# The unit of the attention scores moves into the split of queries and keys; tables are used as loaded

## The chip, the cores and the metric

The kernel runs on one core of one Trainium2 chip. A core has five engines that each follow their own list of instructions in order: TensorE (PE in the profile, with its weight loads as PEld), VectorE (DVE), ScalarE (ACT), GpSimd (POOL) and SyncE (SP), which here issues nearly all DMAs. The metric is device time of one execution in microseconds, the median of the timed runs; lower is better.

## The reference

Two inputs, a prompt of 512 rows and a sample of 1024 rows of width 1024, pass through the same encoder layer. What matters here is its attention part, 8 heads of width 64:

```python
h = rmsnorm(x, n_pre)
aq, ak, av, gq, gk, gv, gr, glr = jnp.split(h @ w_in, IN_OFFSETS, axis=-1)
o_attn = dilated_attention(heads(aq), heads(ak), heads(av))   # three (window, dilation) pairs
#   s = q . k / 8 - slope[h] * |distance|;  softmax of each branch, branches merged by their denominators
o_gla = gla_mixer(gq, gk, gv, gr, glr, ...)                   # gated linear attention beside it
x = x + rmsnorm(concat(o_attn, o_gla) @ w_out, n_post)
# then: h = rmsnorm(x); gelu(depthwise conv(h @ w_up[a])) * (h @ w_up[g]) @ w_down; rmsnorm; residual add
```

The three branches share keys. The kernel computes one softmax over all keys with a table per head that holds slope times distance, less the logarithm of the number of branches that see the key, and 1e30 where none does. Keys that lie outside the sequence, which the reference counts with score zero, enter as one more column, from the table `miss`.

## The kernel before

**Numbers.** A float32 product is made of three products of halves: an operand x becomes hi = fp16(x * f) and lo = fp16(x * f - hi), with a factor f, and `mm3` (lines 343 to 345) adds hi*hi, hi*lo and lo*hi in one PSUM bank. The factors of the weights are powers of two that are measured on the chip: a `Group` of four weight units gets the sum of its squares (`measure`, one ScalarE pass over each unit at line 245), then `finish` makes the factor `scale` with a small TensorE product (line 252), a VectorE sum (253), and GpSimd and VectorE operations on one column. `undo` is what turns a product back into plain numbers; call it u. Queries and keys left the projection as product times the constant `-PART` or `PART` (2 to the -15), so that their product was a score in the unit u * u / PART**2 / 8 of its head pair. The tables of distances and `miss` were divided by that unit on GpSimd, once per head (lines 553 and 556), and the exponential took the unit as its scale, and `top`, the row's extreme times the unit (line 211), as its bias.

**Stages.** The prompt is projected first (`main1`: 12 column blocks in feature-major form, then 6 in token-major form), while the samples' rows are normed beside it. Then the samples are projected (`main2`) while the prompt's attention and linear attention run beside it (`mixers(0, ...)`); then the output projection and the gated MLP of the prompt, with the samples' `mixers(1, ...)` beside the MLP; then the samples' output projection and MLP, which fill the last third of the time. `_weave` sets how many steps of the side work go between the steps of the main work.

**Order.** The program is written as if in one stream, and a scheduler then places each engine's instructions, so that the order on an engine is that of the built program and not of the source. DMAs go out on SP's queue in its order.

**Weights.** `_Weights` takes the weights in units of [128, 512] elements; two units make a load of 512 KB (line 92) into one of six buffers. Before unit i is used, its hi (line 111, ScalarE) and lo (line 120, VectorE) have been made, and the units ahead of it loaded and measured. `ahead(0)`, called with the first row tile, loaded 10 units in five DMAs and measured 8 of them. The first blocks are `inproj_lead`: two blocks by two half-widths, 96 products of 128x256.

**The first rows.** `norm_T` loads a tile of 128 rows, sums its squares (line 368), norms it (398), transposes it on TensorE (405) and splits it into hi and lo, `c` (348 and 353). After the last load come the small tables in SP's order: `gg` (line 1154, a row of 64 numbers spread over 128 partitions and 8 heads), `cf`, which VectorE casts to `cm` (1159), `ph_sb` (the table `miss`), the masks (one of them cast at 1167) and `cvt`.

**Attention.** `attention` handles its heads in a pipeline of steps: `scores` (two matmuls per piece, 583 and 584), one step later `reduce` (VectorE, 597: adds the table to the scores in PSUM, writes `t` and keeps the row's minimum `m`), then `expo` (ScalarE, 610), `part_hi` (reciprocal 618, GpSimd `rs` 619, ScalarE `p` 622), `part_lo` (VectorE, 629), `turn` (a DMA that transposes, 638), `pv` (665) and `out` (674 to 680). `load(h)` brings a head's table (549), queries (559) and keys (561), `load_v` its values; there are two sets of buffers, and head h + 2 is loaded once the scores of head h are reduced. The prompt has 4 row tiles per head and two `t` buffers, the samples 8 and three.

Of the kernel before, what the change touches and what calls it, by code (L numbers as in the profile page):

```python
# [69 lines left out]
class _Weights:  # L70
# [78 lines left out]

    def next(self):  # L150
        i = self.i
        self.flush(i)
        self._finish()
        self._upto("hi", self._hi, i + self.HI)
        self._upto("lo", self._lo, i + self.LO)
        self.ahead(i + 1)
        self.i += 1
        return self.parts.pop(i)
# [3 lines left out]
def encoder(ctx, tc, xp, xs, n_pre, w_in, wg, g_gla, w_out, n_post, n_ffn_pre, w_up, conv, w_down,  # L162
# [65 lines left out]
    class Group:  # L228
# [4 lines left out]
        def __init__(self, nm, n, rows, *more, scores=False):  # L233
# [3 lines left out]
            self.scores = const.tile([128, 3], F32, name=f"scores_{nm}") if scores else None  # L237
# [12 lines left out]
        def finish(self):  # L250
# [10 lines left out]
            if self.scores is not None:  # L261
                c = [self.scores[:, i:i + 1] for i in range(3)]
                times(c[0], u, u)
                times(c[0], c[0], PART ** -2 / 8.0)
                times(c[1], c[0], -1.0)
                nc.vector.reciprocal(out=c[2], in_=c[0])
# [19 lines left out]
    G_FM = [Group(f"fm{i}", 4, r_pre, scores=i < 4) for i in range(6)]  # L286
# [137 lines left out]
    def store_fm(c, i, ps):  # L424
        seq, o0 = where(c)
        m = FM_ORDER[i]
        if m < 8:
            t = tmp.tile([128, 2, CH], FP16, name="stq", tag="two")
            split_psum(ps, t[:, 0], t[:, 1], -PART if m < 4 else PART)
# [105 lines left out]
    def attention(seq):  # L535
# [5 lines left out]
        nbuf = 2  # L541
        with ExitStack() as es:
# [4 lines left out]
            def load(h):  # L547
# [4 lines left out]
                unit = G_FM[h // 2].scores[:, 2:3]  # L552
                nc.gpsimd.tensor_scalar(out=bias, in0=bias, scalar1=unit, scalar2=3e38, op0=ALU.mult, op1=ALU.min)
                miss = hp.tile([128, nkt], F32, name="miss", tag="miss")
                m0 = seq * 32 + h * nkt
                nc.gpsimd.tensor_scalar(out=miss, in0=ph_sb[:, m0:m0 + nkt], scalar1=unit, scalar2=3e38,
                                        op0=ALU.mult, op1=ALU.min)
# [5 lines left out]
                heads[h] = (bias, qs, kk, miss)  # L563
# [15 lines left out]
            def scores(h, qt, k0, k1, last):  # L579
                _, qs, kk, _ = heads[h]  # L580
# [6 lines left out]
            def reduce(h, qt, k0, k1, last):  # L587
                bias, miss = heads[h][0], heads[h][3][:, qt:qt + 1]
# [15 lines left out]
            def expo(h, qt):  # L604
# [3 lines left out]
                s = G_FM[h // 2].scores  # L608
                top = times(up.tile([128, 1], F32, name="top", tag="top", bufs=4), m, s[:, 0:1])
                nc.scalar.activation(out=t[:, kf:], in_=t[:, kf:], func=ACTF.Exp, scale=s[:, 1:2], bias=top,  # L610
                                     accum_out=den)
# [530 lines left out]
    with ExitStack() as es:  # L1142
# [5 lines left out]
        def first():  # L1148
            g_pre.append(gain_row(stage, n_pre, "g0"))
            r_pre.set(g_pre[0])  # L1150
            W.ahead(0)
# [171 lines left out]
```

## Time and profile before

| | us |
|---|---|
| timed runs, median of 3 | 2120.15 (2115.74 to 2127.61) |
| profiled execution | 2108.8 |
| its span, first to last instruction | 2107.0 |
| TensorE busy in it | 1904.1 |
| VectorE, ScalarE, GpSimd busy | 1202.9, 975.8, 373.4 |

The mean granted clock of TensorE over the span was 0.964. The profiled execution was faster than each of the timed ones, so a sum made against its span says by how much the time moves; where the median then lies is read with the 11.35 us between the two in mind. In rows in order of time the first number is the start in us, the second the length of the row's instructions, and what stands in brackets is the idle time of the engine before it and what ended it. In rows of groups, the numbers behind the bar are busy us and mean ns of one, and behind the second bar the idle time before them. Rows by stretch give for each engine the busy us and, in parentheses, the number of instructions.

### The profile page before, as it was taken

Reading aid. Unit: us, or ns where it says so; the run is one execution under the profiler, and the core shown is the slowest. Engines: PE = TensorE matmul, PEld = TensorE weight load, DVE = VectorE, ACT = ScalarE, POOL = GpSimd, SP = SyncE. Lnnn points to the kernel's source line nnn. Section 1 sums busy time; section 2 is a strip of 40 time slices with the busy share of each in tenths; the row PEclk is TensorE's granted clock in tenths of the full one; section 3 lists DMA queues with packets and bytes.
Section 4 is the critical chain, followed back from the end, with each engine's and each line's share of the span. In section 5 each row is a group of like instructions: output and inputs, shape, how many; then the busy total and the mean of one; then the engine's idle time right before and its main releaser. Section 6 shows DMA issues by size and latency. Waiting matters only on the chain. (4 is left out here: it accounts for less than half of the span.)

```text
span 2107.0 us, 31702 instructions
## 1 busy us (share of the span) xinstructions
PE 1904.1 (90%) x11912; PEld 1184.5 (56%) x11912; DVE 1202.9 (57%) x2367; ACT 975.8 (46%) x1858; POOL 373.4 (18%) x657
## 2 busy tenths in 40 slices
PE   3999779999978886799899989989999999999996
PEld 2586334787853443454555557844655656464655
DVE  4554753432448786796756654675254554545456
ACT  5674554322447785686635433553422232314233
POOL 3212540000154443531011111210000000000002
PEclk9999789999999998899999999999999999999998
DMA  6666785335558999985424447641111211111132
GB/s 194 190 181 149 177 177 157 106 102 187 194 151 157 181 174 167 182 175 145 136 86 133 124 162 262 234 162 55 46 46 50 61 40 50 51 55 46 61 125 85
DMA packets 389615, 274.75 MB, mean 130 GB/s; under 512 B 173875, under 2 KB 342067, under 8 KB 389461
## 3 DMA queue, kind: packets, MB, share of 16 engines
q1 hardware_dynamic: 389460, 272.72, 48.1%
q8 instruction: 94, 1.54, 0.3%
q14 instruction: 61, 0.49, 0.1%
HBM read 191.83 MB, written 47.28 MB: 113 GB/s over the span
## 5 line engine op out<-in xcount | busy, mean ns | idle before, releaser
L343 PE MATMUL bank<-c,w_hi 128*128 128x512 f16 (+1 forms) x816 | 313.2, 384 | 16.8 <-ACT w_hi L111 9.4
L345 PE MATMUL bank<-c,w_lo 128*128 128x512 f16 (+1 forms) x816 | 312.0, 383 | 10.3 <-DVE w_lo L120 10.3
L344 PE MATMUL bank<-c,w_hi 128*128 128x512 f16 (+1 forms) x816 | 313.0, 384 | 0.0
L345 PEld LDWEIGHTS <-w_lo 128*128 128x128 f16 x1360 | 135.6, 100 | 175.0 <-DVE w_lo L120 14.5
L343 PEld LDWEIGHTS <-w_hi 128*128 128x128 f16 x1360 | 136.6, 100 | 170.0 <-issue 14.5
L344 PEld LDWEIGHTS <-w_hi 128*128 128x128 f16 x1360 | 135.7, 100 | 162.9 <-issue 19.3
L111 ACT ACTIVATE w_hi<-w_raw,up_up 128x512 f16<-128x512 f32 x176 | 125.6, 720 | 217.0 <-PE bank L344 108.9
L344 PE MATMUL bank<-w_lo,f 128*128 128x512 f32 x528 | 212.9, 403 | 9.5 <-DVE w_lo L118 9.2
L343 PE MATMUL bank<-w_hi,f 128*128 128x512 f32 x528 | 212.2, 409 | 3.1 <-DVE ya L1076 1.7
L345 PE MATMUL bank<-w_hi,f 128*128 128x512 f32 x528 | 211.3, 400 | 0.0
L111 ACT ACTIVATE w_hi<-w_raw 128x512 fp32r<-128x512 f32 x144 | 90.2, 630 | 243.6 <-PE bank L345 190.9
L120 DVE SCALAR_TENSOR_TENSOR w_lo<-w_raw,up_up,w_hi 128x512 f16<-128x512 f32 x176 | 134.6, 767 | 110.5 <-PE bank L345 54.0
L118 DVE TENSOR_TENSOR w_lo<-w_raw,w_hi 128x512 fp32r<-128x512 f32 x144 | 98.5, 688 | 117.2 <-PE bank L344 82.9
L972 POOL TENSOR_TENSOR small<-small 128x1 f32<-128x1 f32 x24 | 8.6, 357 | 812.2 <-ACT junk L368 812.2
L1042 DVE SCALAR_TENSOR_TENSOR ya<-bank,cvt,ya 128x511 f32<-128x511 f32 x176 | 107.9, 614 | 72.8 <-ACT ya L1044 66.6
L1112 DVE TENSOR_TENSOR y<-bank,y 128x512 f32<-128x512 f32 x144 | 96.5, 687 | 87.8 <-PE bank L345 87.6
L345 PE MATMUL bank<-d,w_lo 128*128 128x512 f16 x352 | 133.4, 379 | 1.5 <-DVE w_lo L120 1.5
L343 PE MATMUL bank<-d,w_hi 128*128 128x512 f16 x352 | 133.5, 379 | 0.1
L344 PE MATMUL bank<-d,w_hi 128*128 128x512 f16 x352 | 133.4, 379 | 0.0
L245 ACT ACTIVATE w_junk<-w_raw 128x512 bf16<-128x512 f32 (+1 forms) x136 | 85.3, 627 | 87.3 <-DMA w_raw<-in_w_up_dram 45.7
L344 PEld LDWEIGHTS bank<-w_lo,f 128*128 128x128 f32 x528 | 100.8, 191 | 34.8 <-DVE w_lo L118 13.6
L629 DVE SCALAR_TENSOR_TENSOR p<-t,rs,p 128x512 f16<-128x512 f32 (+2 forms) x96 | 91.2, 955 | 45.1 <-ACT p L622 44.5
(196 smaller groups left out, 3910.5 us busy)
## 6 DMA issues: line engine op xcount, KB each, us to landing
w_raw<-in_w_up_dram SPq DMA_DIRECT2D x88, 512.0 KB, 4.5
w_raw<-in_w_in_dram SPq DMA_DIRECT2D x44, 512.0 KB, 4.4
w_raw<-in_w_down_dram SPq DMA_DIRECT2D x36, 512.0 KB, 3.6
mix<-mx SPq DMA_DIRECT2D x24, 512.0 KB, 10.5
xin<-in_x_sample_dram SPq DMA_DIRECT2D x16, 512.0 KB, 5.1
w_raw<-in_w_out_dram SPq DMA_DIRECT2D x32, 256.0 KB, 6.2
xin<-x SPq DMA_DIRECT2D x16, 512.0 KB, 4.7
bias<-in_nbias_dram SPq DMA_DIRECT2D x8, 832.0 KB, 7.4
```

The costliest lines, as they stand in the source:

```text
L111: self.nc.scalar.activation(out=self.hi[i], in_=raw, func=ACTF.Copy, scale=1.0 if group is None else group.scale)
L118: self.nc.vector.tensor_tensor(out=lo, in0=raw, in1=hi.bitcast(F32), op=ALU.subtract)
L120: self.nc.vector.scalar_tensor_tensor(out=lo, in0=raw, scalar=group.scale, in1=hi, op0=ALU.mult, op1=ALU.subtract)
L245: nc.scalar.activation(out=junk[:, :raw.shape[1]], in_=raw, func=ACTF.Square, accum_out=self.sums[:, self.at:self.at + 1])
L343: nc.tensor.matmul(out, ah, bh, start=start, stop=False)
L344: nc.tensor.matmul(out, ah, bl, start=False, stop=False)
L345: nc.tensor.matmul(out, al, bh, start=False, stop=stop)
L629: nc.vector.scalar_tensor_tensor(out=p[:, n:2 * n], in0=t[:, kf:T], scalar=rs, in1=p[:, 0:n], op0=ALU.mult, op1=ALU.subtract)
L972: nc.gpsimd.tensor_tensor(out=r, in0=self.ss[0], in1=self.ss[1], op=ALU.add)
L1042: nc.vector.scalar_tensor_tensor(out=out, in0=src, scalar=cw[:, j:j + 1], in1=out, op0=ALU.mult, op1=ALU.add)
L1112: nc.vector.tensor_tensor(out=y[t][:, cols], in0=ps[t], in1=y[t][:, cols], op=ALU.add)
```

## The change

Queries and keys now leave the projection with factors of their own head pair in place of the constant: keys with k = min(u, PART), queries with q = -max(u / PART, 1) * u / 8, whose product is -u * u / 8, so that a score comes out in plain numbers (with its sign turned, as before). The tables of distances and `miss` are then used as they are loaded, the exponential has the scale -1.0 and the minimum `m` itself as bias, and the unit, the scaled `miss` tiles and `top` are gone. In the prompt's attention (one chunk) a head's buffers are three in place of two. At the start, `start` loads and measures the four units of the first group only, and makes its factor, with the first row tile; what `ahead(0)` did before is done when the first unit is asked for.

```diff
+    def start(self):
+        n = self.units[0][5].n
+        self._upto("load", self._load, n - 1)
+        self._upto("measure", self._measure, n - 1)
+        self._finish()
+
     def next(self):
         i = self.i
         self.flush(i)
         self._finish()
+        if i == 0:
+            self.ahead(0)
         self._upto("hi", self._hi, i + self.HI)
...
-            self.scores = const.tile([128, 3], F32, name=f"scores_{nm}") if scores else None
+            self.heads = const.tile([128, 2], F32, name=f"heads_{nm}") if heads else None
...
-            if self.scores is not None:
-                c = [self.scores[:, i:i + 1] for i in range(3)]
-                times(c[0], u, u)
-                times(c[0], c[0], PART ** -2 / 8.0)
-                times(c[1], c[0], -1.0)
-                nc.vector.reciprocal(out=c[2], in_=c[0])
+            if self.heads is not None:
+                k, q = (self.heads[:, i:i + 1] for i in range(2))
+                nc.gpsimd.tensor_scalar(out=k, in0=u, scalar1=PART, scalar2=None, op0=ALU.min)
+                nc.gpsimd.tensor_scalar(out=q, in0=u, scalar1=1.0 / PART, scalar2=1.0, op0=ALU.mult, op1=ALU.max)
+                nc.gpsimd.tensor_scalar(out=q, in0=q, scalar1=u, scalar2=-0.125, op0=ALU.mult, op1=ALU.mult)
...
-            split_psum(ps, t[:, 0], t[:, 1], -PART if m < 4 else PART)
+            f = G_FM[i // 2].heads
+            split_psum(ps, t[:, 0], t[:, 1], f[:, 1:2] if m < 4 else f[:, 0:1])
...
-        nbuf = 2
+        nbuf = 3 if nh == 1 else 2
...
                 kk = hp.tile([128, 2, T], FP16, name="kk", tag="kk")
-                unit = G_FM[h // 2].scores[:, 2:3]
-                nc.gpsimd.tensor_scalar(out=bias, in0=bias, scalar1=unit, scalar2=3e38, op0=ALU.mult, op1=ALU.min)
-                miss = hp.tile([128, nkt], F32, name="miss", tag="miss")
-                m0 = seq * 32 + h * nkt
-                nc.gpsimd.tensor_scalar(out=miss, in0=ph_sb[:, m0:m0 + nkt], scalar1=unit, scalar2=3e38,
-                                        op0=ALU.mult, op1=ALU.min)
...
-                bias, miss = heads[h][0], heads[h][3][:, qt:qt + 1]
+                bias = heads[h][0]
+                miss = ph_sb[:, seq * 32 + h * nkt + qt:seq * 32 + h * nkt + qt + 1]
...
-                s = G_FM[h // 2].scores
-                top = times(up.tile([128, 1], F32, name="top", tag="top", bufs=4), m, s[:, 0:1])
-                nc.scalar.activation(out=t[:, kf:], in_=t[:, kf:], func=ACTF.Exp, scale=s[:, 1:2], bias=top,
-                                     accum_out=den)
+                nc.scalar.activation(out=t[:, kf:], in_=t[:, kf:], func=ACTF.Exp, scale=-1.0, bias=m, accum_out=den)
...
             r_pre.set(g_pre[0])
-            W.ahead(0)
+            W.start()
```

The scheduler moves instructions with it. On GpSimd, in the prompt's attention, this is where the first heads end (`rs` is the probability factor, `t` gets the `miss` column, and line numbers of the changed kernel are higher by one to nine). Before:

```order
L211 TENSOR_SCALAR top<-m,scores_fm_129 128x1
L556 TENSOR_SCALAR miss<-ph_sb,scores_fm_132 128x4
L211 TENSOR_SCALAR top<-m,scores_fm_129 128x1
L619 TENSOR_SCALAR rs<-rs 128x1 x2
L591 COPY t<-miss 128x1 x2
L211 TENSOR_SCALAR top<-m,scores_fm_129 128x1
L553 TENSOR_SCALAR bias<-bias,scores_fm_132 128x1152
L619 TENSOR_SCALAR rs<-rs 128x1
L211 TENSOR_SCALAR top<-m,scores_fm_129 128x1
L591 COPY t<-miss 128x1
```

and now:

```order
L476 TENSOR_TENSOR stg<-stg,gg 128x256 x4
L620 TENSOR_SCALAR rs<-rs 128x1 x2
L595 COPY t<-ph_sb 128x1 x2
L620 TENSOR_SCALAR rs<-rs 128x1 x2
L595 COPY t<-ph_sb 128x1 x2
L620 TENSOR_SCALAR rs<-rs 128x1
L595 COPY t<-ph_sb 128x1
```

Only `rs` and the copies of one column are left, and no instruction there waits for a table.

On SP, from the program's start. Before:

```order
L390 DMA xin<-in_x_prompt_dram 128x1024
L272 DMA g_209<-in_norm_mix_pre_dram 128x1024
L92 DMA w_raw<-in_w_in_dram 128x8x128 x5
L390 DMA xin<-in_x_prompt_dram 128x1024 x3
L1154 DMA gg<-in_gla_norm_dram 128x8x64
L1158 DMA cf<-in_cums_dram 128x264
```

and now:

```order
L398 DMA xin<-in_x_prompt_dram 128x1024
L280 DMA g_209<-in_norm_mix_pre_dram 128x1024
L92 DMA w_raw<-in_w_in_dram 128x8x128 x2
L398 DMA xin<-in_x_prompt_dram 128x1024 x3
L1155 DMA gg<-in_gla_norm_dram 128x8x64
L1159 DMA cf<-in_cums_dram 128x264
L1162 DMA ph_sb<-in_miss_dram 128x96
L1164 DMA diag_340<-in_masks_dram 128x64
L1167 DMA mf<-in_masks_dram 128x64
L1170 DMA cvt<-in_conv_dram 128x88
L92 DMA w_raw<-in_w_in_dram 128x8x128 x3
```

Three of the five weight loads moved from ahead of the row tiles to behind the small tables.

On VectorE, in the same place. Before, after the norms and splits of all four row tiles (`small<-bank` sums a group's squares, `up_fm` is its factor):

```order
L1159 CAST cm<-cf 128x264
L1167 CAST after_mask<-mf 128x64
L253 TENSOR_REDUCE small<-bank 128x1 x2
L207 TENSOR_SCALAR up_fm_130<-up_fm_130 128x1
L207 TENSOR_SCALAR up_fm_133<-up_fm_133 128x1
```

and now:

```order
L262 TENSOR_REDUCE small<-bank 128x1
L216 TENSOR_SCALAR up_fm_130<-up_fm_130 128x1
L266 RECIPROCAL undo_fm_131<-undo_fm_131 128x1
L406 SCALAR_TENSOR_TENSOR xin<-xin,small,g_209 128x1024
L120 SCALAR_TENSOR_TENSOR w_lo<-w_raw,up_fm_130,w_hi 128x512
L406 SCALAR_TENSOR_TENSOR xin<-xin,small,g_209 128x1024
L1160 CAST cm<-cf 128x264
L120 SCALAR_TENSOR_TENSOR w_lo<-w_raw,up_fm_130,w_hi 128x512
L361 SCALAR_TENSOR_TENSOR c<-bank,rows_pre,c 128x4x128 x2
L406 SCALAR_TENSOR_TENSOR xin<-xin,small,g_209 128x1024
L361 SCALAR_TENSOR_TENSOR c<-bank,rows_pre,c 128x4x128 x2
```

The first group's factor and the first `w_lo` moved ahead of the first splits `c`, and so did the cast that waits for `cf`.

More of the change, by code (lines that the diff above doesn't have):

```diff
@@ L228, in encoder, with __init__ @@
     class Group:
-        def __init__(self, nm, n, rows, *more, scores=False):
+        def __init__(self, nm, n, rows, *more, heads=False):
             self.n, self.rows, self.more, self.at = n, rows, more, 0
-            self.scores = const.tile([128, 3], F32, name=f"scores_{nm}") if scores else None
+            self.heads = const.tile([128, 2], F32, name=f"heads_{nm}") if heads else None
             self.scale = const.tile([128, 1], F32, name=f"up_{nm}")
@@ L285, in encoder @@
     TM = [(O_V, 256), (O_V + 256, 256), (O_GV, 256), (O_GV + 256, 256), (O_GR, 256), (O_GR + 256, 272)]
-    G_FM = [Group(f"fm{i}", 4, r_pre, scores=i < 4) for i in range(6)]
+    G_FM = [Group(f"fm{i}", 4, r_pre, heads=i < 4) for i in range(6)]
     G_TM = [Group(f"tm{i}", 4, r_pre, (1.0 / PART / P_SCALE, None, 0.5)[i // 2]) for i in range(6)]
@@ L562, in load @@
                                       in_=QK[seq][4 + h // 2][:, r, :].rearrange("s p t -> p s t"))
-                heads[h] = (bias, qs, kk, miss)
+                heads[h] = (bias, qs, kk)
             def load_v(h):
@@ L579, in scores @@
             def scores(h, qt, k0, k1, last):
-                _, qs, kk, _ = heads[h]
+                _, qs, kk = heads[h]
                 ps = bank()
```

## The prediction

> **What bounds the kernel now.** I read the page first, then busy time by stage, then the waits, then the order of time around the longest TensorE gaps. The profiled execution took 2108.8 us around a span of 2107.0 us; the three timed runs have a median of 2120.15 us, 11.35 us more. The sum below is made against 2108.8, and 11.35 us is added at its end.
>
> ```profile
> span 2107.0 us, 31702 instructions
> PE 1904.1 (90%) x11912; PEld 1184.5 (56%) x11912; DVE 1202.9 (57%) x2367; ACT 975.8 (46%) x1858; POOL 373.4 (18%) x657
> ```
>
> TensorE (PE) is busy for 90%, so at most 203 us of idle time can go, plus what a lower granted clock costs. The stages (columns: stretch, its length, busy time of each engine, granted clock PEclk, share of the DMA engines, GB/s) tell where that is:
>
> ```profile
> 60.00:189.00 129.00, 127.10 (x916) 90.04 (x914) 63.02 (x111) 80.60 (x165) 25.72 (x54) 1.00 0.61 182
> 189.00:330.00 141.00, 114.37 (x543) 55.27 (x542) 90.54 (x221) 77.66 (x157) 57.83 (x106) 0.87 0.82 174
> 640.00:960.00 320.00, 258.19 (x1287) 146.38 (x1286) 249.38 (x588) 231.24 (x426) 135.14 (x248) 0.92 0.91 173
> 1400.00:2107.00 707.00, 690.67 (x3114) 399.71 (x3111) 370.01 (x573) 221.09 (x357) 12.88 (x24) 0.99 0.19 59
> ```
>
> The change touches the start (0 to 60) and the two attention stages (189 to 330 for the prompt, 573 to 960 for the samples). There TensorE is idle 26.6 us in 141 and 61.8 us in 320, at a granted clock of 0.87 and 0.92. The last 707 us run at 98% and are not touched.
>
> What stalls attention is one long GpSimd instruction per head, the scaling of the distance table:
>
> ```profile
> L553 POOL TENSOR_SCALAR bias<-bias,scores_fm 128x1152 f32<-128x1152 f32 (+1 forms) x16 | 85.0, 5309 | 34.3 <-DMA bias<-in_nbias_dram 33.8
> L211 POOL TENSOR_SCALAR top<-m,scores_fm 128x1 f32<-128x1 f32 x96 | 46.4, 484 | 48.0 <-DVE m L597 44.4 <-DVE rs L618 3.2 <-DVE undo_up L257 0.2
> ```
>
> It does harm in two ways. First, GpSimd runs in order: it waits for the table to land and then scales it, and the small `rs` behind it (L619), which a probability tile needs, comes late. In order of time:
>
> ```profile
> 208.85 4.22 POOL L553 TENSOR_SCALAR bias<-bias,scores_fm 128x1152 f32<-128x1152 f32 x1 [5.76 <-DMA bias<-in_nbias_dram]
> 213.15 0.23 POOL L619 TENSOR_SCALAR rs<-rs 128x1 f32<-128x1 f32 x1
> 215.88 1.87 PE L665 MATMUL bank<-pt,v 128*128 128x256 f16 x8 [5.45 <-DVE m L597]
> ```
>
> Second, VectorE instructions with two operands in SBUF stretch while it runs: the same `o` subtraction takes 4.00 us beside the scaling at 225.00 and 0.41 us without it, and in the start two `w_lo`, 767 ns on the mean elsewhere, take 5.01 us together; TensorE waits 6.18 us for them:
>
> ```profile
> 225.00 4.22 POOL L553 TENSOR_SCALAR bias<-bias,scores_fm 128x1152 f32<-128x1152 f32 x1 [1.74 <-DMA bias<-in_nbias_dram]
> 225.13 4.00 DVE L678 TENSOR_TENSOR o<-oa,o 64x256 fp32r<-64x256 f32 x1
> 236.69 0.41 DVE L678 TENSOR_TENSOR o<-oa,o 64x256 fp32r<-64x256 f32 x1
> L120 DVE SCALAR_TENSOR_TENSOR w_lo<-w_raw,up_up,w_hi 128x512 f16<-128x512 f32 x176 | 134.6, 767 | 110.5 <-PE bank L345 54.0 <-PE bank L344 27.9 <-issue 27.2
> 47.13 5.32 POOL L553 TENSOR_SCALAR bias<-bias,scores_fm 128x1152 f32<-128x1152 f32 x1
> 48.27 5.01 DVE L120 SCALAR_TENSOR_TENSOR w_lo<-w_raw,up_fm,w_hi 128x512 f16<-128x512 f32 x2
> 52.67 0.39 PE L345 MATMUL bank<-c,w_lo 128*128 128x256 f16 x1 [6.18 <-DVE w_lo L120]
> ```
>
> **The change, part by part.** *Tables as loaded.* All 16 scalings (85.0 us of GpSimd), 16 `miss` and 96 `top` (46.4 us) go. What they cost TensorE I take from the stretches around the stalls with a scaling in their chain. For the prompt these are four, from 208 to 303.3: the first, then the sum of the four, then the sum of their parts at half clock. Below, the same for the samples' five, from 619 to 897.3:
>
> ```profile
> 208.00:224.80 16.80, 7.98 (x25) 3.33 (x25) 8.39 (x22) 8.97 (x18) 7.67 (x14) 0.59 0.70 169
> sum 54.40, PE 28.23 PEld 11.87 DVE 32.95 ACT 29.40 POOL 27.23; mean PE 7.06 PEld 2.97 DVE 8.24 ACT 7.35 POOL 6.81
> sum 37.60, PE 22.60 PEld 9.44 DVE 27.30 ACT 23.88 POOL 17.07; mean PE 5.65 PEld 2.36 DVE 6.83 ACT 5.97 POOL 4.27
> ```
>
> ```profile
> 619.00:627.60 8.60, 4.04 (x19) 1.99 (x17) 4.87 (x8) 2.40 (x7) 7.51 (x9) 0.80 0.25 67
> sum 49.40, PE 30.22 PEld 14.96 DVE 32.96 ACT 27.24 POOL 27.46; mean PE 6.04 PEld 2.99 DVE 6.59 ACT 5.45 POOL 5.49
> sum 24.60, PE 20.43 PEld 9.66 DVE 18.95 ACT 17.19 POOL 12.30; mean PE 4.09 PEld 1.93 DVE 3.79 ACT 3.44 POOL 2.46
> ```
>
> Prompt: idle 54.40 - 28.23 = 26.2 us, and 22.60 us of matmuls at half clock, of which half is lost, 11.3: 37.5 us at most. Samples: 19.2 + 10.2 = 29.4 us at most. The lower end is nothing, if another wait takes each place. For the prompt I take three quarters, 28 us, since between the stalls TensorE does not idle with the same attention beside it:
>
> ```profile
> 259.00:276.00 17.00, 17.00 (x93) 8.77 (x92) 11.39 (x33) 9.97 (x20) 6.74 (x16) 1.00 1.09 193
> ```
>
> For the samples I take six tenths, 17.5 us: their DMA share is 0.91, and other waits stand there that the change leaves (weights from HBM and transposes):
>
> ```profile
> ACT w_junk L245 <- DMA w_raw<-in_w_up_dram: 45.7, 19, 7.8
> PE bank L665 <- DMA pt<-p: 10.1, 4, 3.5
> ```
>
> A rule of the Trainium skill would price the clock lower: in TensorE: Matmul & The Clock Gate, Part 1, about 3.4 us without work halve the clock and about 3.4 us of work restore it, so each stall would cost some 1.7 us of clock, nine of them 15.3 us as an estimate instead of 21.5, and the sum would shrink by about 4 us. Here the prompt's four stretches at half clock add up to 37.6 us, 9.4 us each and not 3.4, since shorter gaps follow the first; the rows decide.
>
> *Score unit in the split factors.* 24 ScalarE and 24 VectorE instructions on `stq` read their factor from a column in place of a constant. The nearest rows with a column are `c`:
>
> ```profile
> L348 ACT ACTIVATE stq<-bank 128x512 f16<-128x512 f32 x24 | 14.0, 585 | 6.5 <-PE bank L345 6.4
> L348 ACT ACTIVATE c<-bank,rows_fpre 128x512 f16<-128x512 f32 x16 | 10.2, 680 | 1.1 <-PE bank L405 1.0
> ```
>
> 24 x 95 ns = 2.3 us of ScalarE, beside matmuls while ScalarE is busy 80.6 us of 129: nothing on the path, 2.3 us if that cover were gone. The exponential loses a column as its scale and its wait for `top`; that is in the stalls above.
>
> *Third head buffer (prompt).* Each table and its keys are wanted one head later than they are loaded, so the wait for landing leaves the path too. It adds one head's loads to the time before attention. SP waits there until a stored query or key block has landed before it can issue the next weight load; one such wait stands in the trace, from 63.86 to 69.63, and TensorE idled 1.90 us some 6 us later. Three heads can make that three: -4 us, between 0 and twice that.
>
> ```profile
> 63.28 0.58 SPq L92 DMA_DIRECT2D w_raw<-in_w_in_dram  x1
> 69.63 1.96 SPq L561 DMA_DIRECT2D kk<-qk  x3
> 77.39 0.39 PE L345 MATMUL bank<-c,w_lo 128*128 128x512 f16 x1 [1.90 <-DVE w_lo L120]
> ```
>
> *First weights with the first row tile.* Two weight loads instead of five go ahead of the prompt's other row tiles, and the first group's scale is ready before them. But the new order puts the cast of `cm`, which waits for `cf`, ahead of the first activation splits, and `cf` lies behind `gg`, during which the DMA engines are nearly idle:
>
> ```profile
> 6.00:15.00 9.00, 1.97 (x8) 1.57 (x8) 4.16 (x6) 5.82 (x16) 1.49 (x4) 1.00 1.16 301
> 20.00:28.00 8.00, 6.53 (x28) 5.67 (x28) 6.47 (x9) 5.24 (x8) 2.92 (x4) 1.00 0.08 22
> 23.23 1.28 DVE L398 SCALAR_TENSOR_TENSOR xin<-xin,small,g 128x1024 f32<-128x1024 f32 x1 [0.71 <-POOL small L358]
> 24.43 4.28 DVE L353 SCALAR_TENSOR_TENSOR c<-bank,rows_pre,c 128x512 f16<-128x512 f32 x6
> 32.23 0.30 DVE L1159 CAST cm<-cf 128x264 fp32r<-128x264 f32 x1 [3.52 <-DMA cf<-in_cums_dram]
> 37.39 0.42 PE L344 MATMUL bank<-c,w_hi 128*128 128x256 f16 x1
> 50.70:57.60 6.90, 4.92 (x24) 3.50 (x25) 4.48 (x5) 0.23 (x1) 6.64 (x4) 0.51 0.38 114
> ```
>
> Three loads of 512 KB at 301 GB/s are 5.2 us, so `cf` lands near 27.0. Behind the cast on VectorE stand one `w_lo` (0.77), four `c` splits (4.28 / 6 each, 2.9) and one norm (1.28), and TensorE waits for all of them: with the cast (0.30) 5.3 us, so the first full products start near 32.3 instead of 37.4, 5 us. Then the 6.18 us gap and half of the 4.92 us of matmuls at half clock behind it, 2.5, have no cause left: at most 8.7 us. I take 6.5. The next three weight tiles now lie behind `gg` and the small tables: they land at 1.74 us each from about 27, with the two behind them by 36, and the measuring of these now stands ahead of the second group's `w_hi` on ScalarE. In the old run the first group's products ran from 37.2 to 46.5 (52.67 - 6.18), 9.3 us, and 24 of 96 were still to come; from 32.3 on the same work lasts to about 44, so this fits, with less in hand than before. On GpSimd two copies from `ph_sb`, which lands with `cf`, stand ahead of the third norm's root: no later than the cast.
>
> Sum: 28 + 17.5 + 5 + 6.5 - 4 = 53 us. 2108.8 - 53 = 2055.8 us beside the profile, 2067 us beside the median of 2120.
>
> **Rivals.** (a) *The stalls become DMA waits.* SP issues transposes, loads and stores in one order, and attention cannot exceed the DMA share of 0.91 that the samples' stage holds over 320 us. The prompt's stage holds 0.82 x 141 = 116 us of DMA work, which then takes 127: a gain of 14, none for the samples. With 7.5 from the start: 21 us, 2099. For it speaks the share of 0.91; against it the 1.09 from 259 to 276 at full TensorE. (b) *The GpSimd work was hidden* and only the start gains: 7.5 us, 2113, no change. The scaling at 225.00 does leave TensorE busy; the one at 208.85 does not. (c) *Slower: the prompt's projection becomes bound by loads.* Two weight tiles go ahead instead of five. The prompt's projection takes 24 loads of two units; each of the 22 after the first two could show its latency in the stage from 60 to 189:
>
> ```profile
> w_raw<-in_w_in_dram SPq DMA_DIRECT2D x44, 512.0 KB, 4.4
> ```
>
> 22 x 4.4 = 97 us, 2164. From 12 shown loads on (53 us) the gain is gone, from 15 on it is slower. Against it: the stage has a DMA share of 0.61, and the order of loading from the third step on is as before.
>
> **How the numbers follow.** The forecast has 0.70, (a) 0.17, (b) 0.08, (c) 0.05. 0.5% is 10.6 us, about what a measurement of this kernel can tell from no change. Faster: the forecast and most of (a), 0.84; the same: (b) and the rest of (a), 0.11; slower: 0.05. With every term in full (37.5 + 29.4 + 5 + 8.7 = 80.6) it would be 2040; the upper end takes in (a) and a little beyond. Range 2038 to 2104.
>
> **What would show it.** GpSimd at 373 - 85 - 46 = 242 us or below; no VectorE `o` or `w_lo` of 2 us or more in attention; TensorE idle under 10 us from the prompt's attention start to its end, with a granted clock near 0.97; the first full product near 32 us and no 6 us gap behind it. Wrong it would be if the waits of L583 and L665 came back on transposes or keys at the same size, or if gaps before `w_lo` appeared in the projection.

## The result and the profile after

The changed kernel takes 2063.78 us, the median of four runs (2059.53 to 2070.07), against 2121.62 us for the kernel before, measured beside it: a ratio of 0.973, with a 95% interval of 0.969 to 0.977, or 57 us less (49 to 66). The profiled execution took 2070.07 us, the longest of the four, around a span of 2068.3 us:

```profile
span 2068.3 us, 31548 instructions
PE 1896.9 (92%) x11912; PEld 1186.7 (57%) x11912; DVE 1176.3 (57%) x2363; ACT 967.9 (47%) x1858; POOL 239.7 (12%) x529
```

GpSimd's 373.4 us became 239.7, TensorE is as busy as before, and 38.7 us of span are gone. To see where, both traces are cut at the same six pieces of work, whose ends lie at other times now: the first product with a `w_lo`, the prompt's first score matmul, its last product with `v`, the samples' first score matmul, their last product with `v`, and the end. Busy time by stretch (columns as in the prediction: length, busy us of each engine, granted clock, DMA share, GB/s), before:

```profile
0.00:38.00 38.00, 9.12 (x39) 7.38 (x40) 14.91 (x29) 20.12 (x42) 9.42 (x27) 1.00 0.72 222
38.00:189.10 151.10, 143.02 (x1018) 101.91 (x1019) 75.40 (x124) 90.02 (x186) 41.35 (x70) 0.98 0.57 173
189.10:327.10 138.00, 111.37 (x528) 53.84 (x527) 88.79 (x217) 76.24 (x154) 57.83 (x106) 0.86 0.82 173
327.10:628.80 301.70, 277.40 (x2552) 208.00 (x2551) 120.68 (x243) 110.43 (x225) 47.55 (x57) 0.97 0.47 147
628.80:964.70 335.90, 273.04 (x1356) 153.22 (x1355) 259.84 (x611) 240.85 (x446) 137.41 (x256) 0.92 0.89 172
964.70:2107.00 1142.30, 1090.12 (x6427) 660.14 (x6425) 643.31 (x1145) 438.12 (x808) 79.87 (x143) 0.99 0.31 100
```

and of the changed kernel:

```profile
0.00:31.90 31.90, 6.69 (x28) 5.63 (x29) 11.04 (x19) 14.31 (x27) 7.95 (x22) 0.90 0.66 197
31.90:183.30 151.40, 146.18 (x1031) 103.39 (x1029) 73.57 (x130) 95.39 (x201) 32.67 (x70) 0.97 0.65 194
183.30:304.10 120.80, 106.21 (x529) 52.55 (x528) 80.19 (x217) 75.18 (x154) 16.50 (x63) 0.93 0.96 189
304.10:600.70 296.60, 275.60 (x2551) 209.23 (x2549) 116.29 (x242) 110.19 (x224) 32.91 (x51) 0.97 0.48 149
600.70:915.10 314.40, 263.58 (x1356) 151.01 (x1355) 250.96 (x610) 234.11 (x447) 69.09 (x180) 0.93 0.97 184
915.10:2068.30 1153.20, 1098.61 (x6427) 664.85 (x6425) 644.23 (x1146) 438.68 (x809) 80.63 (x143) 0.98 0.31 99
```

The start is 6.1 us shorter, the prompt's attention 17.2, the stretch to the samples' attention 5.1 (the first two of the samples' scalings lay there), the samples' attention 21.5. The prompt's projection gained nothing in this trace. The last piece, which the change does not touch, is 10.9 us longer with the same 6427 matmuls: their busy time rose by 8.5 us with the lower granted clock. So the two profiled executions understate the gain: up to the last piece it is 49.6 us. In the runs below this last piece takes 1143 to 1155 us, which is the noise that a comparison of two single traces carries.

The stretched VectorE instructions are gone. This is the view of one line of the changed kernel (shortest, median and longest, in ns); `o` took up to 4.00 us before:

```profile
L679 DVE TENSOR_TENSOR o<-oa,o x48: 408/417/419, 215.8 to 917.3; 64x256 fp32r<-64x256 f32 x48
```

What TensorE still waits for in the prompt's attention, before and then after (us in all, times, longest):

```profile
PE bank L583 <- DVE m L597: 14.0, 5, 5.8
PE bank L665 <- DVE m L597: 8.5, 2, 5.5
```

```profile
PE bank L586 <- DVE m L601: 9.1, 4, 3.6
PE bank L666 <- DVE m L601: 3.2, 2, 2.1
```

They are the same waits, for VectorE to empty a bank, at about half the size. In the start, in order of time on VectorE, TensorE and ScalarE of the changed kernel:

```profile
26.35 0.30 DVE L1160 CAST cm<-cf 128x264 fp32r<-128x264 f32 x1 [6.48 <-DMA cf<-in_cums_dram]
29.97 1.94 PE L413 MATMUL bank<-idt,xin 128*128 128x128 f32 x8 [7.84 <-DVE xin L406]
31.70 0.42 PE L352 MATMUL bank<-c,w_hi 128*128 128x256 f16 x1
62.04 0.63 ACT L254 ACTIVATE w_junk<-w_raw 128x512 bf16<-128x512 f32 x1 [4.01 <-DMA w_raw<-in_w_in_dram]
67.37 0.61 PE L353 MATMUL bank<-c,w_lo 128*128 128x512 f16 x1 [3.34 <-DVE w_lo L120]
```

The cast waits for `cf` to 26.35, and the first full product starts at 31.70. The 6.18 us gap behind the first group is gone, but a new one of 3.34 us stands at 64.0, behind a wait of ScalarE for a weight load that SP issued at 53.69, after the stores of the first query blocks.

### The profile page after: what moved, and what is told of

It is laid out like the page before. It is cut to its first block, busy times and chain, and to the rows that moved or that the text cites. A ratio compares the mean times of both kernels' runs of the same rounds, so it can differ in the third digit from the quotient of the medians.

```text
span 2068.3 us, 31548 instructions
## 1 busy us (share of the span) xinstructions
PE 1896.9 (92%) x11912; PEld 1186.7 (57%) x11912; DVE 1176.3 (57%) x2363; ACT 967.9 (47%) x1858; POOL 239.7 (12%) x529
## 5 line engine op out<-in xcount | busy, mean ns | idle before, releaser
L351 PEld LDWEIGHTS bank<-w_hi,f 128*128 128x128 f32 x528 | 100.7, 191 | 27.6 <-ACT w_hi L111 1.5
```

The source lines that it names most:

```text
L351: nc.tensor.matmul(out, ah, bh, start=start, stop=False)
```

## The experiments

All ratios are to the kernel before, measured beside each run. The table gives them with their 95% intervals, and the lengths of the six pieces in us in the profiled execution of each run, cut as above.

| run | ratio (95%) | start | projection | prompt att. | between | samples' att. | rest |
|---|---|---|---|---|---|---|---|
| before | 1 | 38.0 | 151.1 | 138.0 | 301.7 | 335.9 | 1142.3 |
| changed | 0.973 (0.969 to 0.977) | 31.9 | 151.4 | 120.8 | 296.6 | 314.4 | 1153.2 |
| e1 tables only | 0.976 (0.973 to 0.979) | 38.0 | 145.9 | 121.3 | 294.1 | 312.6 | 1147.6 |
| e2 start only | 0.993 (0.991 to 0.996) | 31.9 | 148.6 | 137.2 | 300.8 | 336.3 | 1147.7 |
| e3 two head buffers | 0.974 (0.971 to 0.977) | 31.8 | 147.6 | 122.3 | 298.3 | 314.8 | 1152.9 |
| e4 third buffer only | 0.998 (0.996 to 1.001) | 38.1 | 153.8 | 134.2 | 302.3 | 331.6 | 1148.6 |
| e5 full scaling back | 0.996 (0.994 to 0.998) | 31.7 | 153.3 | 133.0 | 309.5 | 333.9 | 1145.3 |
| e6 one column | 0.973 (0.971 to 0.976) | 31.9 | 145.2 | 121.1 | 294.3 | 317.5 | 1145.1 |
| e7 spare tile | 0.992 (0.989 to 0.994) | 32.0 | 146.6 | 134.2 | 297.7 | 337.7 | 1146.2 |
| e8 top back | 0.979 (0.976 to 0.983) | 31.4 | 147.6 | 123.5 | 297.1 | 315.3 | 1152.3 |
| e9 VectorE delay | 0.981 (0.979 to 0.984) | 31.5 | 145.5 | 118.1 | 293.2 | 329.7 | 1154.5 |
| e10 gg later | 0.973 (0.971 to 0.975) | 24.8 | 153.1 | 119.4 | 300.8 | 318.3 | 1148.5 |
| e11 seven weight buffers | 0.971 (0.968 to 0.973) | 31.5 | 149.1 | 117.9 | 294.7 | 311.8 | 1143.0 |
| e12 seven, gg later still | 0.974 (0.971 to 0.976) | 24.7 | 159.2 | 117.5 | 292.8 | 315.0 | 1151.8 |

### One part of the change at a time

**Tables only** (e1): the changed kernel with the old buffers and the old start.

```diff
-        nbuf = 3 if nh == 1 else 2
+        nbuf = 2
...
-            W.start()
+            W.ahead(0)
```

> The kernel before with one part of the change: the score unit in the split factors and the tables used as loaded; two head buffers and the old start stay. Theory (the prediction's own terms): 28 us of the prompt's attention and 17.5 us of the samples' go, 45 us, so the ratio to the kernel before is near 0.979. Rival (the GpSimd work was hidden, the gain of 58 us comes from start and buffers): within 10 us of the kernel before, ratio 0.995 to 1.005.

Measured 0.976, 51 us: the theory. By pieces it is 16.7 us in the prompt's attention, 7.6 and 23.3 us up to and in the samples' attention, and 5.2 us in the projection, where the gap behind the first products shrank from 6.18 to 2.53 us:

```profile
49.33 0.28 PE L353 MATMUL bank<-c,w_lo 128*128 128x256 f16 x1 [2.53 <-DVE w_lo L120]
```

**Start only** (e2): the kernel before with `start` and the call of `ahead(0)` in `next`.

```diff
-            W.ahead(0)
+            W.start()
```

> The kernel before with one part of the change: the first group's weights loaded and measured with the first row tile; scalings and two head buffers stay. Theory: the first full products start 5 to 6 us earlier; of the 6.5 us for the gap behind them little comes, since the scalings that stretch the two w_lo are still there, so 5 us, ratio 0.998. Rival (the gap was the start order's doing and not the scalings'): 11 us, ratio 0.995.

Measured 0.993, 14 us: more than the theory, and the rival's 11 lies in its interval. The start is 6.1 us shorter and the gap behind it is gone, with the scalings still in place. One of them still stretches a VectorE instruction, but in the new order it is a norm of a sample's tile, which nobody is waiting for yet, and no `w_lo`:

```profile
50.30 4.20 DVE L407 SCALAR_TENSOR_TENSOR xin<-xin,small,g 128x1024 f32<-128x1024 f32 x1
```

So the new order takes this gap away, and the tables as loaded most of it. That would explain why 51 and 14 us, 65 together, are 56 us in one kernel (e3); the three intervals are so wide that they leave about these 9 us open.

**Two head buffers** (e3), the changed kernel without the third buffer, and **third buffer only** (e4), the kernel before with it:

```diff
-        nbuf = 3 if nh == 1 else 2
+        nbuf = 2
```

> The changed kernel with two head buffers in the prompt's attention. Theory of the prediction (the third buffer costs 4 us of landing waits ahead of attention and brings nothing of its own): 4 us faster than the changed kernel, ratio to the kernel before 0.971. Rival (the third buffer takes waits for tables and keys out of the prompt's attention): slower than the changed kernel by 5 us or more, ratio 0.976 or above, with waits of the scores' matmuls for keys in its trace.

> The kernel before with one part of the change: three head buffers in the prompt's attention; scalings and old start stay. Theory (the stalls come from GpSimd waiting in order for a table and from its length, which a third buffer leaves as they are): within 5 us of the kernel before, ratio 0.998 to 1.003, the scalings still ahead of rs and the stalls of 5 us still there. Rival (a table that comes one head earlier takes the wait away, and the third buffer alone brings the prompt's gain): 15 us or more, ratio 0.993 or below.

Without the third buffer the changed kernel takes the same time, 0.974 against 0.973; the kernel before with it takes 0.998, with an interval that holds 1. In single traces the prompt's attention is 1.5 and 3.8 us shorter with three buffers, and the projection is 3.8 and 2.7 us longer. But of the first 3.8 us of projection, 3.4 are matmuls at a lower granted clock: TensorE is busy for 146.18 us at 0.97 in the changed kernel, and with two buffers for

```profile
31.80:179.40 147.60, 142.77 (x1031) 101.88 (x1029) 73.75 (x130) 95.27 (x200) 32.68 (x70) 1.00 0.64 191
```

Its idle time there grows by 0.4 us with the third buffer, and by 1.0 us in the second pair. A loss of 4 us lies outside the interval of e4. Between the changed kernel and e3 it is not excluded, and a gain of 5 us is excluded in neither pair. The new 3.34 us gap at 64.0 is not the third buffer's: with two buffers the projection has a gap of 2.91 us at 63.4.

### What about the scaling cost the time

Four kernels, all the changed kernel with two head buffers, put one thing back each. In the first the full operation stands where it was (e5), in the second it covers one column (e6), so that GpSimd still waits for the table but is soon done; in the third an operation of the old length, at another place, works on a tile that no DMA writes (e7); in the fourth only `top` is back (e8).

The full operation (`one` is a column of 1.0):

```diff
                 nc.sync.dma_start(out=bias, in_=nbias[h, :, 0:bw])
+                nc.gpsimd.tensor_scalar(out=bias, in0=bias, scalar1=one, scalar2=3e38, op0=ALU.mult, op1=ALU.min)
```

> The changed kernel with two head buffers, and the 16 GpSimd operations over the whole distance table put back at their old place, with a factor of 1.0 (its values stay); top and the scaled miss tiles stay out. Between the kernel with scalings and the new start (ratio 0.9932) and the changed kernel with two buffers (0.9737) lie 41 us. Theory (the scalings carry the stalls): 30 to 41 us come back, ratio 0.988 to 0.993. Rival (top, 96 GpSimd operations between the row's minimum and the exponential, carries them): less than 15 us come back, ratio below 0.981.

One column:

```diff
                 nc.sync.dma_start(out=bias, in_=nbias[h, :, 0:bw])
+                nc.gpsimd.tensor_scalar(out=bias[:, 0:1], in0=bias[:, 0:1], scalar1=one, scalar2=3e38, op0=ALU.mult, op1=ALU.min)
```

> As the run before, but the operation covers one column of the table: GpSimd waits for the table as long as before, and then is busy for some 0.2 to 0.5 us in place of 4.2 to 5.3. Theory A (the stall is GpSimd waiting in order for the table, with rs behind it): at least two thirds of what the full scaling cost comes back, 20 to 28 us, ratio 0.983 to 0.987. Theory B (the stall is the length of the operation and its stretching of VectorE): less than a third, ratio below 0.979.

The spare tile `loose`:

```diff
                 nc.gpsimd.tensor_scalar(out=rs, in0=rs, scalar1=P_SCALE, scalar2=None, op0=ALU.mult)
+                if qt == 1:
+                    nc.gpsimd.tensor_scalar(out=loose[:, 0:bw], in0=loose[:, 0:bw], scalar1=rs, scalar2=3e38,
+                                            op0=ALU.mult, op1=ALU.min)
```

> The changed kernel with two head buffers and 16 GpSimd operations of the old length, once per head behind the second rs, on a tile that no DMA writes and nobody reads: the length and the stretching without the wait for a table. Theory A (the wait): less than a third of the full scaling's cost, ratio below 0.979. Theory B (length and stretching): two thirds or more, ratio 0.984 to 0.990.

And `top`:

```diff
-                nc.scalar.activation(out=t[:, kf:], in_=t[:, kf:], func=ACTF.Exp, scale=-1.0, bias=m, accum_out=den)
+                top = times(up.tile([128, 1], F32, name="top", tag="top", bufs=4), m, one)
+                nc.scalar.activation(out=t[:, kf:], in_=t[:, kf:], func=ACTF.Exp, scale=-1.0, bias=top, accum_out=den)
```

> The changed kernel with two head buffers, and the 96 small GpSimd operations top put back between the row's minimum and the exponential, with a factor of 1.0. The prediction costed them only as part of the stalls. Theory (an operation of 0.48 us in the pipeline's step is hidden, since the exponential comes a step after the minimum): within 5 us of the kernel without them, ratio 0.972 to 0.976. Rival (the chain minimum, top, exponential is on the path in places where VectorE is late): 10 us or more, ratio 0.978 or above.

The full scaling brings 0.0221 back, 47 us: the scalings carry the whole loss, somewhat more than the theory's 41. The one column brings nothing back (0.9732 against 0.9737), although GpSimd waits for the tables in it as much as with the full operation, 52.5 us against 50.0. From the view of its line, with what GpSimd waited for:

```profile
L561 POOL TENSOR_SCALAR bias<-bias,one x16: 291/292/1391, 49.1 to 836.0; 128x1 f32<-128x1 f32 x16
...
  DMA bias<-in_nbias_dram: 52.5, 13
```

and its two attention stages, then those with the spare tile:

```profile
177.10:298.20 121.10, 104.59 (x529) 51.84 (x528) 79.39 (x217) 75.08 (x154) 19.32 (x68) 0.96 1.00 198
592.50:910.00 317.50, 266.39 (x1356) 152.17 (x1355) 250.97 (x610) 233.93 (x447) 69.38 (x186) 0.91 0.97 182
```

```profile
178.60:312.80 134.20, 109.44 (x528) 53.15 (x527) 98.56 (x217) 75.24 (x154) 49.74 (x70) 0.91 0.88 178
610.50:948.20 337.70, 273.20 (x1356) 154.54 (x1355) 276.22 (x610) 234.51 (x447) 115.56 (x188) 0.90 0.89 171
```

Without any table to wait for, the long operation brings 0.018 back, 38 us. Theory B holds: it was the length of the operation, and the wait for the table alone cost nothing. That e5 costs more than e7 fits their places, by the pieces of the traces: in the two attention stages its 12 operations add 29.8 us to e3's, and the 16 of e7 add 34.8; its other four lie ahead of these stages and add 16.9 there, where e7 has none. With the long operation the DMA share of the samples' attention falls from 0.97 to 0.89 again: the low share was an effect of the stalls.

Both of the ways that the prediction named are in the trace, and at the same places. In order of time on GpSimd, VectorE, ScalarE and TensorE, with the spare tile: behind one operation a `w_lo` on VectorE takes 3.84 us in place of 0.74, while ScalarE waits 2.89 us for the `rs` that stands behind the operation, and TensorE idles 2.46 us for a bank that VectorE empties late. Behind another a `p` on VectorE takes 3.27 us in place of 0.75, `rs` comes at 237.85, and TensorE idles 5.40.

```profile
215.25 4.22 POOL L625 TENSOR_SCALAR loose<-loose,rs 128x1152 f32<-128x1152 f32 x1
215.81 3.84 DVE L120 SCALAR_TENSOR_TENSOR w_lo<-w_raw,up_fm,w_hi 128x512 f16<-128x512 f32 x1
219.55 0.23 POOL L623 TENSOR_SCALAR rs<-rs 128x1 f32<-128x1 f32 x1
219.81 0.72 ACT L629 ACTIVATE p<-t,rs 128x512 f16<-128x512 f32 x1 [2.89 <-POOL rs L623]
221.91 1.50 PE L672 MATMUL bank<-pt,v 128*128 128x256 f16 x8 [2.46 <-DVE m L604]
```

```profile
233.56 4.22 POOL L625 TENSOR_SCALAR loose<-loose,rs 128x1152 f32<-128x1152 f32 x1
234.68 3.27 DVE L636 SCALAR_TENSOR_TENSOR p<-t,rs,p 128x512 f16<-128x512 f32 x1 [0.81 <-ACT p L629]
238.78 1.01 PE L672 MATMUL bank<-pt,v 128*128 128x256 f16 x4 [5.40 <-DVE m L604]
```

How much of the idle time each of the two costs cannot be read from these places. In the kernel before, at the scaling at 208.85 that the prediction shows, the late `rs` acts alone, by the operation's wait for its table and its length together: ScalarE waits 8.77 us for it, VectorE idles 9.55 us for the `p` that ScalarE makes with it, and no VectorE instruction there is stretched.

The stretched `p` ends at 237.95, 0.17 us after the GpSimd operation (237.78), and the `w_lo` 0.18 us after its own. With its usual 0.75 us taken off, `p` would have begun 0.58 us before that operation's end; the same sum gives 0.56 for the `w_lo`, 0.58 for the norm of e2 (beside an operation from 49.03 to 53.80) and 0.50 for the `o` that the prediction shows. So each did its work close to the operation's end, whenever it had started. The Trainium skill gives the mechanism in SBUF — State Buffer, SBUF: two separate sides: VectorE, in an instruction with two inputs in SBUF, and GpSimd share a pair of ports under an exclusive lock that one instruction holds to its end, while the other waits. The rows here agree with a hold up to about half a microsecond before the end, and not with a sharing.

`top` put back gives 0.979, which is the rival's figure (0.978 or above), 12 us more than e3. But the interval overlaps with that of e3, and the two attention stages, where `top` acts, are only 1.2 and 0.5 us longer in the trace. With the 47 us of the scalings, 12 us would also be more than the 41 that both should share. What `top` costs stays open.

**VectorE delay** (e9). With the spare tile VectorE was 45 us busier than without (1221.0 against 1175.7). Here it gets two operations of its own per head instead, and GpSimd none.

```diff
+                if qt == 1:
+                    for _ in range(2):
+                        nc.vector.scalar_tensor_tensor(out=loose, in0=loose, scalar=den, in1=loose,
+                                                       op0=ALU.mult, op1=ALU.min)
                 nc.vector.reciprocal(out=rs, in_=den)
```

> The changed kernel with two head buffers, and two VectorE operations of 128x1108 per head, ahead of the second reciprocal, on a tile that nobody else reads: some 2.8 us of VectorE time per head, 44 us in all, as much as the 16 GpSimd operations on the spare tile added to VectorE's instructions by stretching them. GpSimd is left free. Theory (the stretched VectorE instructions are what stalls TensorE): 28 us or more of the spare tile's 38 come back, ratio 0.987 or above. Rival (rs and the miss column, held up on GpSimd behind the long operation, are what stalls it): under 13 us, ratio below 0.980.

Measured 0.981, between the two: 16 us of the spare tile's 38.

```profile
177.00:295.10 118.10, 104.49 (x530) 51.22 (x529) 98.67 (x235) 74.72 (x155) 24.60 (x62) 0.97 1.00 203
588.30:918.00 329.70, 268.84 (x1356) 150.49 (x1355) 271.06 (x626) 235.50 (x446) 67.92 (x180) 0.92 0.91 175
```

The two stages differ. In the prompt VectorE is as busy as with the spare tile (98.67 and 98.56 us), but the stage takes 118.1 us (122.3 in e3) and not 134.2: VectorE's time as such costs nothing there. What is left is that the long operation holds `rs` back on GpSimd, or that it holds one VectorE instruction for 3 to 4 us in one piece, where the delay here comes in pieces of 1.37 us; this was not told apart. In the samples' attention, where VectorE is busy for 80% of the time before anything is added, 20 us more of it cost 15 us of the stage's time.

### The start, and weights further ahead

**gg later** (e10): its load stands behind the small tables and three weight loads. **Seven weight buffers** (e11): weights are loaded one load further ahead. **Both, gg later still** (e12): behind the first four sample tiles.

Of the load of `gg`, in e10:

```diff
-        nc.sync.dma_start(out=gg.rearrange("p (h v) -> p h v", h=HEADS),
-                          in_=g_gla.unsqueeze(0).unsqueeze(0).to_broadcast([128, HEADS, DH]))
...
         def side1():
+            nc.sync.dma_start(out=gg.rearrange("p (h v) -> p h v", h=HEADS),
+                              in_=g_gla.unsqueeze(0).unsqueeze(0).to_broadcast([128, HEADS, DH]))
             yield from norm_T(x_tiles(1), g_pre, r_pre, h1)
```

In e12 it stands behind that `norm_T` instead. Of the weights, in e11 and e12:

```diff
-    LOAD, SCALE, HI, LO = 1, 2, 3, 2
+    LOAD, SCALE, HI, LO = 3, 2, 3, 2
...
-        t = self.pool.tile([128, 2 * self.width], F32, name="w_raw", tag="w_raw", bufs=6)
+        t = self.pool.tile([128, 2 * self.width], F32, name="w_raw", tag="w_raw", bufs=7)
```

> The changed kernel with the load of gg behind the small tables and the next three weight loads. In the changed kernel's trace the cast of cm waits 6.48 us for cf, to 26.35, the third norm is behind it, and TensorE idles 7.84 us for that norm. Theory (gg holds up cf, as the prediction's start term has it): cf lands near 20.5, the first full product starts 5 to 6 us earlier, near 26.5, and the time is 5 us below the changed kernel's, ratio 0.9705. Rival (norms and splits on VectorE and the roots on GpSimd bound the start by themselves): first full product at 30 or later, ratio 0.973.

> The changed kernel with seven weight buffers in place of six, and weights loaded one load (two units) further ahead. In the changed kernel's trace ScalarE waits 98.6 us in all for weight loads before it can measure them, and the TensorE gaps of 5.4 us at 562.5 and 5.0 us at 579.8 stand in the stage of these waits. Theory (a load one step earlier takes the waits away): 10 to 20 us below the changed kernel, ratio 0.964 to 0.968. Rival (the DMA engines, at a share of 0.92 in the samples' attention, deliver no earlier whatever the order): ratio 0.971 to 0.975.

> The changed kernel with seven weight buffers and weights loaded one load further ahead, as before, and gg loaded behind the first four sample tiles, so that no weight load of the first groups lies behind it. With gg behind three weight loads the first full product started at 24.8 in place of 31.9, but the measuring of the next weights waited 4.14 us for a load that lay behind gg, and TensorE idled 4.10 us at 33.6. Theory (that load was what took the start's gain back): first full product near 25, no gap of 4 us up to 60 us, and 6 to 8 us below the kernel with seven buffers alone (ratio 0.9707), so 0.967 to 0.968. Rival (the products run ahead of what ScalarE can measure and split in any order): gaps of 4 us or more between 25 and 60 us stay, ratio 0.970 or above.

With `gg` later the start is 7.1 us shorter, as the theory has it, and the time is the same (0.973): the projection is longer by 1.7 us in that trace, and by 5.5 against e3. ScalarE now waits for the weight load that lies behind `gg`, and in e12 for another one; the DMA engines are nearly idle in both places. First e10, then e12:

```profile
36.20 0.63 ACT L254 ACTIVATE w_junk<-w_raw 128x512 bf16<-128x512 f32 x1 [4.14 <-DMA w_raw<-in_w_in_dram]
24.00:28.00 4.00, 4.00 (x27) 3.18 (x25) 3.01 (x4) 3.47 (x8) 0.00 (x0) 1.00 0.07 18
```

```profile
55.84 0.63 ACT L254 ACTIVATE w_junk<-w_raw 128x512 bf16<-128x512 f32 x1 [10.82 <-DMA w_raw<-in_w_in_dram]
44.00:48.00 4.00, 4.00 (x21) 1.78 (x19) 2.14 (x4) 0.82 (x3) 0.00 (x0) 1.00 0.07 19
```

So the theory behind e12 falls: the start is as short as it says, and its gaps, 2.23 us at 27.9 and 2.14, 1.41 and 1.22 us between 55 and 66, are smaller than the rival's 4 us, but the projection is longer by 10 us than with seven buffers alone and the gain does not come. At each of the places that were tried, the 256 KB of `gg` run at a DMA share of about 0.07 for 8 us or more, and the loads behind them come late.

Seven buffers give 0.971, 5 us less than the changed kernel by the ratios, and 2051 us, the lowest median of all; the intervals overlap, so that it is better is not shown. The waits of ScalarE before it measures weights did shrink, from the changed kernel's

```profile
ACT w_junk L254 <- DMA w_raw<-in_w_up_dram: 51.8, 22, 8.8
ACT w_junk L254 <- DMA w_raw<-in_w_in_dram: 46.8, 13, 6.4
```

to

```profile
ACT w_junk L254 <- DMA w_raw<-in_w_in_dram: 38.2, 11, 6.7
ACT w_junk L254 <- DMA w_raw<-in_w_up_dram: 35.6, 21, 5.6
```

that is by 24.8 us, and the samples' attention is 2.6 us shorter: most of these waits were not on the path, and the 10 to 20 us expected do not come.

## Why the prediction was right, and where it was not

The time came out where the forecast had it, 2063.78 us for 2067, and the largest term had the right sign and, summed over both attentions, nearly the right size. By its steps:

- **Tables as loaded, 28 + 17.5 = 45.5 us.** Tables alone brought 51 us, 5.2 of them in the projection, with the gap behind the first products. Term by term the sizes were off in opposite directions: the prompt's attention gave 17.2 us (16.7 in e1) where 28 were taken, the samples' 21.5 us and 5.1 ahead of it (23.3 and 7.6 in e1) where 17.5 were. For the prompt the mis-sized step is "three quarters, since between the stalls TensorE does not idle". It does once the stalls are gone: it still waits 12.3 us for VectorE to empty banks, of 22.5 before. For the samples the cut to six tenths, for a DMA share of 0.91 and other waits, was wrong: the share rose to 0.97, and about the whole 29.4 us of the stalls' price came (26.6, and 30.9 in e1).
- **The two harms of the scaling.** "GpSimd waits for the table to land and then scales it": only the second half counts. The wait alone costs nothing (e6); the length does (e7). It holds back what is queued behind it on GpSimd and holds a VectorE instruction, as the prediction says; how the cost splits between the two was not told apart.
- **Factor column, nothing.** The split on ScalarE takes 672 ns by the median where it took 580, 2.2 us in all for the 2.3 worked out, and VectorE's half 62 ns more, which had not been counted; no run isolated it.

```profile
L356 ACT ACTIVATE stq<-bank,heads_fm x24: 665/672/687, 45.1 to 310.0; 128x512 f16<-128x512 f32 x24
L361 DVE SCALAR_TENSOR_TENSOR stq<-bank,heads_fm,stq x24: 736/748/753, 49.4 to 310.7; 128x512 f16<-128x512 f32 x24
```

- **Third head buffer, -4 us.** Not seen (e3, e4). TensorE's idle time in the projection grows by 0.4 and 1.0 us with it and not by 4, and the gap put down to such waits stands with two buffers too.
- **Start, 5 us.** Right by its own steps: `cf` cast at 26.35 where 27.0 was worked out, first product at 31.70 for 32.3, 6.1 us gained.
- **The gap behind the start, 6.5 us.** The gap went, but its cause was only half named: the prediction puts it down to the scalings, though its rival (b) counts the 6.5 us to the start. The new order alone removes it (e2), the tables alone leave 2.53 us of it (e1). In the changed kernel's trace the projection is 151.4 us long after 151.1, so that nothing of the 6.5 us is left; with two head buffers it is 145.2 to 147.6 us long (e3 and e6 to e9), 3.5 to 5.9 us less than before. What took the gain back in the changed kernel's trace is mostly half clock, up to 35.5 us and behind the new gap of 3.34 us:

```profile
25.20:35.50 10.30, 5.53 (x26) 4.64 (x27) 7.40 (x11) 3.93 (x8) 2.09 (x5) 0.50 1.10 305
66.20:73.00 6.80, 5.63 (x17) 2.96 (x18) 6.36 (x10) 5.21 (x11) 1.44 (x2) 0.50 0.48 154
```

  The three loads that the prediction saw come closer are not the late ones. It judged that "this fits", and it did: TensorE idles at most 0.89 us in one piece from 31.7 to 64.0. The late load is one that SP issued at 53.69, after the stores of the first query blocks, and that landed near 62.0, 8.3 us later, where 4.4 us was the median in the kernel before. The prediction has no term for it, and why it took so long was not tested.
- **What would show it.** GpSimd at 239.7 (at most 242), no stretched `o`, first product at 31.70, no 6 us gap: as said. TensorE idle in the prompt's attention is 14.6 us (120.80 - 106.21) and not under 10, at a clock of 0.93 and not 0.97. One of its signs of being wrong did appear: a gap ahead of a `w_lo` in the projection, the 3.34 us. The other did not: the waits that are left in the prompt's attention are for VectorE and not for transposes or keys.
- **Rivals.** (a) falls: the DMA share goes to 0.96 and 0.97, and a share seen beside stalls was no limit. (b) falls with e1 and e5. (c) falls in size, though its kind of wait is there: 4.01 us at 62.04.

That the total came this close is luck in good part: by the pieces of the changed kernel's trace the forecast has 11 us too many in the prompt's attention and 3 in the projection, and 9 us too few for the samples and 1 in the start, and these nearly cancel.

## What to carry to other kernels

In these runs a long operation, on an engine that shares an order with small ones and a port with another engine, cost by its length, and where something that was wanted stood behind it: a one-column operation with the same wait was free, and 16 operations of 4.2 to 7.0 us cost 47 us. So before such work is hidden elsewhere, see if it can be moved into a factor that is applied anyway. And a busy share that was measured beside stalls says little on the limit of that resource, as a stretch without waits says little on what waits once the large stalls are gone.

## What was not expected of the hardware

- **The load that runs at almost no rate.** `gg`, 64 numbers spread over 128 partitions and 8 heads, keeps the share of the DMA engines at 0.07 (18 to 19 GB/s) and loads behind it in the same queue come late, at each of three places in the program: waits of 6.48 us in the changed kernel, 4.14 in e10 and 10.82 in e12. Loading one row and copying it on the chip was not tried.
- **Half a clock without a long pause.** TensorE's clock fell to half after 3.4 us in which it was busy for 1.84 us, with no gap longer than 1.2 us, and stayed there for twice that time while TensorE was fully busy. From busy time by stretch of the changed kernel:

```profile
407.60:411.00 3.40, 1.84 (x16) 1.23 (x13) 1.23 (x1) 1.06 (x1) 0.00 (x0) 0.99 0.55 196
411.00:414.40 3.40, 3.40 (x16) 3.17 (x17) 0.69 (x4) 2.53 (x8) 0.00 (x0) 0.50 0.00 0
414.40:417.80 3.40, 3.40 (x18) 2.38 (x16) 2.38 (x5) 0.05 (x1) 0.00 (x0) 0.50 0.02 5
```

  It cost 3.4 us for 1.6 us of idle time. The rule that the prediction weighed (the Trainium skill, TensorE: Matmul & The Clock Gate, Part 1: about 3.4 us without work halve the clock, at least about 3.4 us of work restore it) does not foresee this fall, ahead of which no pause of 3.4 us stands; the 6.8 us to the return are twice the least time that it gives.
